# The first attention head and its value block are loaded ahead of the attention section, and the planner prices a transfer by its bytes

## The chip, the cores and the metric

The kernel runs on one core of a Trainium2 chip. The metric is device time in microseconds (us) of one launch, the median of several runs. The engines named below are TensorE (PE: matrix products and transposes), VectorE (DVE), ScalarE (ACT), GpSimd (POOL) and SyncE (SP), which here only issues transfers (DMAs) between the chip's memory and the on-chip buffers. Each engine works through its own instructions strictly in program order, and so does SP's list of transfers.

## What is computed

One layer of a decoder, on 16 learned tokens and 1024 tokens of width 1024. Cut to what the change touches:

```python
h = rms_norm(concat(meta_tokens, x), g_pre_mix) @ w_in          # 8 blocks of 1024 features
b_c, c_c, h_c, q, k, v, g_conv, g_attn = split(h)
branch_conv = (b_c * causal_dwconv(c_c * h_c)) @ w_proj_conv
# stick-breaking attention, 16 heads of 64 features, query blocks of 128
z    = q_block @ k.T / 8
beta = log_sigmoid(z)
fail = where(s < t, beta - z, 0)
a    = where(s < t, exp(beta + reverse_cumsum(fail) - fail), 0)
branch_attn = concat(a @ v) @ w_proj_attn
merged = sigmoid(g_conv + b0) * branch_conv + sigmoid(g_attn + b1) * branch_attn
h = h + rms_norm(merged @ w_out, g_post_mix)
# then a gated MLP with a depthwise convolution, and its own norms
```

Every product is done in float32 accuracy from split operands: a matrix is rounded to a high part, the rest is kept as a low part, and three matmuls (high by high, high by low, low by high) make one product.

## The kernel before

**Stages.** A short prologue normalises and turns the tokens into features (`xnT`). The *projection section* then makes the feature blocks of `w_in`, 128 features at a time: some blocks plainly, 21 pairs of blocks by a Strassen-like scheme with seven products on halves, for which four sums of token halves are kept split in the tiles T1 to T4 (`tpool`). Queries, keys and values go to the chip's memory (`qh_d`, `ql_d`, `kh_d`, `kl_d`, `vv_d`), and later come back one head at a time. The last block of this section is the *bridge*: one gate block (`bridge_gate`), done plainly, 72 matmuls from `xnT` alone. The *attention section* works through 8 pairs of heads, and 12 more gate blocks (`mid_gates`) are threaded between as filler for TensorE. The output projections and the MLP follow.

**Attention, per head.** A head's queries and keys (`qh`, `ql`, `kk`) are six transfers of 64 rows; a pair's values (`vv`) are two transfers. For nine query blocks in three groups: scores `z` (PE, two matmuls for a chunk), `fl` = sigmoid(-z) (ACT, L970), a scan along the keys (DVE, L981), transposes `tp` (PE, L1000), a high part `ah` (ACT, L1005) and a low part `al` (DVE, L447), and the weighted values `av` (PE, L1015 and L1016).

**A gate block** needs its weights: a transfer `raw` (L358), a cast `whi` on ACT (L457), a low part `wlo` on POOL (L369), then 72 matmuls (L345 to L347) in three chunks, each ended by a sigmoid on ACT (L670) into `gt`; the whole is stored by SP (L673).

**What sets the order.** Both sections are written through a planner (`Plan`): tasks with an engine, a cost, a key, dependences and slots (buffers). It plays them through with those costs; whenever an engine is free it takes the ready task with the lowest key, and the instructions are emitted in that order and then held to it. The costs thus decide only which instruction stands before which. Before the change each SP task cost 0.4, a head 2.4 and a value block 0.8, with a lag of 3.5 until its data counts as there. The projection section and the attention section are two separate plans, and each starts with an idle SP.

**Buffers around the change.** The pool `heads` (three buffers each of `qh`, `ql`, `kk`, two of `vv`) is opened where the tiles T1 to T4 lay, after the first plan was emitted. The pool `work`, with the `fl` tiles, is opened where the projection section's ring of output tiles (`su`, `hi`, `gt`) lay; a tile of `work` may be written only when the stores that read the old tile there have ended.

The plan's first gate after the bridge (`nxt`, i = 0 of the mid gates) has its weights loaded and split in the projection section already. Below it is *gate 0*; *gate 1* is the first whose `raw` is loaded in the attention section.

Of the kernel before, what the change touches and what calls it, by code (L numbers as in the profile page):

```python
# [11 lines left out]
F32 = mybir.dt.float32  # L12
# [5 lines left out]
P = 128  # L18
D = 1024
# [14 lines left out]


class Plan:
    LAG = {"PE": 0.22, "ACT": 0.18, "DVE": 0.13, "POOL": 0.13, "SP": 3.5, None: 0.0}

    def __init__(self, slots):
        self.slots = dict(slots, port=1)  # L40
# [89 lines left out]

def any_cost(n):
    return {"DVE": dve_cost(n), "POOL": pool_cost(n)}


@with_exitstack
def block_kernel(ctx, tc, x, meta_tokens, g_pre_mix, w_in, channels, w_proj_conv,
# [312 lines left out]
    def plain(o, chunks, key, make, evac, finish, psum, first_chunk=0, given=None, eng="ANY"):  # L449
        st = {}  # L450
        if given is None:
            def load():
                st["raw"] = load_raw(o)

            def high():
                st["hi"], st["lo"] = whole(st["raw"])
                nc.scalar.copy(st["hi"], st["raw"])  # L457

            ld = plan.add("SP", 0.4, load, key=key - 16, takes=("raw",))
            h = plan.add("ACT", act_cost(D), high, (ld,), key - 10, ("whi", "wlo"))  # L460
            los = [plan.add(eng, any_cost(512) if eng == "ANY" else pool_cost(512),
                            lambda e="POOL", i=i: lo_piece(st["raw"], st["hi"], st["lo"], i, e, 512), (h,),
                            key - 9 + 3 * i) for i in range(2)]
            plan.join(los, ("raw",))
        else:
            st["hi"], st["lo"], los = given
        before, evacs = None, []
        for ci in range(first_chunk, 3):
            a, n = chunks[ci]
# [58 lines left out]
    def done_b(cb, u, after, key):  # L528
        y, after2 = mixed.pop(("y", cb))

        def product(e):
            engine_of(e).tensor_tensor(y()[:, :NQ], y()[:, :NQ], u()[:, T0:], op=ALU.mult)

        t = plan.add("ANY", any_cost(NQ), product, tuple(after) + tuple(after2), key + 4)
        plan.join((t,), ("wk",))
        plan.add("SP", 0.4, lambda: nc.sync.dma_start(y_d[cb * P:(cb + 1) * P, :], y()[:, :NQ]),
                 (t,), key + 5, (), ("wk",))

    def done_qk(hi_d, lo_d, t0):
        def done(p, u, after, key):  # L540
# [6 lines left out]
            def lower(e):  # L547
# [4 lines left out]
            s1 = plan.add("SP", 0.4, lambda: nc.sync.dma_start(hi_d[rows, :], st["hi"].bitcast(F32)), (h,), key + 4)  # L552
            plan.join((s1, t), ("wk",))
            plan.add("SP", 0.4, lambda: nc.sync.dma_start(lo_d[rows, :], u()[:, t0:]),
                     (t,), key + 5, (), ("wk",))
        return done

    def done_v(p, u, after, key):
# [15 lines left out]
        for k0, kn, m in ((0, 4, P), (4, 4, P), (8, 1, QB)):  # L574
# [28 lines left out]
            plan.add("SP", 0.4, store, (w,), key + 7, (), ("wk",))  # L603
        plan.join(turned, ("wk",))

    def token_op(name, kb, a, n):
# [56 lines left out]
    def gate_out(which, ob, tile_of, space):  # L663
        u = {}

        def make():
            u["t"] = tile_of()

        def evac(a, n, ps):
            nc.scalar.activation(u["t"][:, a - T0:a - T0 + n], ps, AF.Sigmoid, bias=bias_gate(which, ob))  # L670

        def finish(after, key):
            plan.add("SP", 0.4, lambda: nc.sync.dma_start(  # L673
                (gc_d, ga_d)[which][ob * P:(ob + 1) * P, :], u["t"][:, :NQ]), tuple(after), key, (), space)
        return make, evac, finish

# [54 lines left out]
    def strassen_pair(i, at):  # L731
# [14 lines left out]
        ld = [plan.add("SP", 0.4, lambda j=j: load(j), (), at - 30, ("raw",)) for j in range(2)]  # L746

        def keep(name, src, after):
            def high():
# [82 lines left out]
        for k in range(7):  # L832
            pair = []
            for s in range(2):
# [18 lines left out]
                else:  # L853
                    p[6, s] = product(6, s, "b1", False, "T4", (p["e", s],))
                    evac(s, 1, 0, "b1", None, (p[6, s],), p[6, s].key, ("st",))
            plan.join((p[k, 0], p[k, 1]), (tags[names[k]],))
        for o in range(2):
            _, k, done = pairs1[i][o]
            done(k, late_tile(u[o]), evacs[o], at + (12 + o) * prod)

    snap_free = {}
    for i in range(len(pairs1)):
        strassen_pair(i, at)
        at += 14 * prod
# [14 lines left out]
    ld = plan.add("SP", 0.4, next_load, (), at - 20, ("raw",))  # L879
# [14 lines left out]
    heads_ctx = ctx.enter_context(ExitStack())  # L894
    heads = heads_ctx.enter_context(pool("heads", 3))
    work_ctx = ctx.enter_context(ExitStack())
    work = work_ctx.enter_context(pool("work", 2, "right"))
    upper = work.tile([QB, NT], F32, name="upper", tag="upper", bufs=1)
# [2 lines left out]
                            compare_op=ALU.is_gt, fill=1.0, base=0, channel_multiplier=1)  # L901

    FL = [2] * 6 + [1] * 3
    plan = Plan({"raw": 2, "whi": 1, "wlo": 1, "mm": 2, "z": 2, "tp": 3, "av": 1, "qk": 3, "vv": 2,
                 "ot": 2, "wk": 2, "ah": 4, "al": 4, "half": 1, **{f"fl{b}": n for b, n in enumerate(FL)}})
    plan_bank = "mm"
    units = [(p, h, g) for p in range(NPAIR) for h in range(2) for g in range(3)]
# [5 lines left out]
        starts[u] = t  # L913
        t += share[u[2]] * half_pair
    DELAY = 0.6 * half_pair
    vload, out_tiles = {}, {}
    av_last = last_turn = None
    for p in range(NPAIR):
        ot_parts = []
        vst = {}  # L920

        def load_v(p=p, vst=vst):
            vst["vv"] = heads.tile([P, 9, 2, P], F32R, name="vv", tag="vv", bufs=2)
            nc.sync.dma_start(vst["vv"][:, 0:8].bitcast(F32), vv_d[p, :, 0:8])
            nc.sync.dma_start(vst["vv"][:QB, 8:9].bitcast(F32), vv_d[p, :QB, 8:9])

        v_ld = None
        v_users = []
        for h in range(2):
            hst = {}  # L930

            def load_h(p=p, h=h, hst=hst):
                r = slice(p * P + 64 * h, p * P + 64 * h + 64)
                qh, ql = (heads.tile([P, NQ], F32R, name=n, tag=n) for n in ("qh", "ql"))
                kk = heads.tile([P, NT], F32R, name="kk", tag="kk")
                for z0 in (0, 64):
                    zs = slice(z0, z0 + 64)
                    nc.sync.dma_start(qh[zs].bitcast(F32), qh_d[r, :])
                    nc.sync.dma_start(kk[zs].bitcast(F32), (kl_d if z0 else kh_d)[r, :])
                    nc.sync.dma_start(ql[zs].bitcast(F32), ql_d[r, :])  # L940
                hst["q"] = (qh, ql, kk)

            t_h = starts[p, h, 0]
            h_ld = plan.add("SP", 2.4, load_h, (), t_h - 40, ("qk",))
            if h == 0:
                v_ld = plan.add("SP", 0.8, load_v, (), t_h - 35, ("vv",))
            z_users = []
            for g in range(3):
                t_u = starts[p, h, g]
                scans, fls = {}, {}  # L950
                for b in range(3 * g, 3 * g + 3):
# [6 lines left out]
                    while c0 < nk:  # L958
                        n = min(wch, nk - c0)

                        def scores(c0=c0, n=n, q0=q0, bst=bst, hst=hst):
                            qh, ql, kk = hst["q"]
                            z = bst["z", c0] = ps_z.tile([P, 512], F32, name="z", tag="z")[:QB, :n]
                            nc.tensor.matmul(z, qh[:, q0:q0 + QB], kk[:, c0:c0 + n], start=True, stop=False)
                            nc.tensor.matmul(z, ql[:, q0:q0 + QB], kk[:, c0:c0 + n], start=False, stop=True)
# [23 lines left out]
                for kb in range(nkb):  # L989
# [21 lines left out]
                    def weigh(kb=kb, n=n, off=off, h=h, nkb=nkb, kst=kst, ust=ust, vst=vst):  # L1011
                        if kb == 0:
                            ust["av"] = ps_av.tile([P, 512], F32, name="av", tag="av")[:, :CH]
                        av, w = ust["av"], vst["vv"][:n, kb, h, :]
                        nc.tensor.matmul(av[:, off:], w, kst["ah"][:n, off:], start=(kb == 0), stop=False)  # L1015
                        nc.tensor.matmul(av[:, off:], w, kst["al"][:n, off:], start=False,  # L1016
                                         stop=(kb == nkb - 1))
# [38 lines left out]
        def last_add(e="POOL", p=p):  # L1056
# [4 lines left out]
        plan.add("SP", 0.4, lambda p=p: nc.sync.dma_start(o_d[p * P:(p + 1) * P, :], out_tiles[p][:, :NQ]),  # L1061
                 (fin,), t_o + 1, (), ("ot",))

    for i, (which, ob) in enumerate(mid_gates):
# [721 lines left out]
```

## Time and profile before

| | |
|---|---|
| time, median of 3 runs | 2003.27 us (2003.04 to 2005.58) |
| the profiled execution's own time | 2005.19 us |
| its span, first to last instruction | 2003.3 us |
| mean granted TensorE clock | 0.987 |
| projection section ends (bridge's last matmul) | 551.0 us into the span |
| last product of the attention section | about 970 us |

The profile is one execution. Busy PE includes the pipeline depth of each matmul, so in a dense stretch records overlap and the spacing of their starts (0.16 us for a matmul of 342 columns) is the pace. The view of waits lists idle time of an engine by what ended it. The view by stretches gives busy time per engine, the granted clock (1.00 is full speed) and how busy the 16 DMA engines were. The timeline gives instructions by start; SPq is SP's issue of a transfer, not the transfer.

### The profile page before, as it was taken

The numbers are of one execution on the slowest core, as the hardware profiler recorded it, in microseconds if no ns is written. First come the engines' busy times: TensorE is split into PE (matmuls) and PEld (weight loads), VectorE is DVE, ScalarE is ACT, GpSimd is POOL, SyncE is SP. The second block draws the span as 40 slices with busy tenths as digits, with TensorE's granted clock in tenths as the row PEclk, the third lists the DMA queues.
The fourth block names the chain that finished last, engine by engine and source line by source line (L and its number), as shares of the span: only waits on it lengthen the run. The fifth ranks groups of instructions, "written<-read, shape, count | busy, mean of one in ns | idle before, by whom it ended". The sixth has DMA issues, their size and how long they took to land.

```text
span 2003.3 us, 32045 instructions
## 1 busy us (share of the span) xinstructions
PE 1922.9 (96%) x12732; PEld 1809.7 (90%) x12732; DVE 1129.5 (56%) x1730; ACT 838.2 (42%) x1766; POOL 646.9 (32%) x486
## 2 busy tenths in 40 slices
PE   6999999999959999999899999989999999999997
PEld 6999999999959999999799999879988998888886
DVE  6846666655428878787541126874444444355547
ACT  5533343444326667666531223453443344321122
POOL 1110000001112323223223550354656465654353
PEclk9999999999979999999999999999999999999999
DMA  3522221455575554541484673213222222253224
GB/s 139 163 85 75 75 75 50 143 153 158 145 197 142 127 148 130 140 130 43 147 241 155 197 196 113 89 44 112 77 72 81 88 79 70 95 177 107 84 85 136
DMA packets 73842, 238.55 MB, mean 119 GB/s; under 512 B 15401, under 2 KB 17225, under 8 KB 72669
## 3 DMA queue, kind: packets, MB, share of 16 engines
q1 hardware_dynamic: 70368, 226.00, 37.6%
q10 hardware_dynamic: 3324, 10.50, 1.7%
q8 instruction: 100, 1.64, 0.4%
q14 instruction: 50, 0.40, 0.1%
HBM read 166.02 MB, written 70.46 MB: 118 GB/s over the span
## 4 chain that ended last, share of the span: by engine, by line
PE 76%; DVE 10%; DMA 6%; ACT 3%; POOL 3%; issue 2%; SPq 0%; ACTq 0%; DVEq 0%; POOLq 0%
PE st L798 7%; PE st L795 7%; PE st L797 7%; PE st L1402 6%; PE st L1406 5%; PE st L1404 5%; DVE fl L981 3%; PE st L1696 3%; PE st L1694 3%; PE st L1695 3%; PE tp L1000 2%; PE mm L245 2%; PE mm L246 2%; PE mm L247 2%; PE mm L345 2%
## 5 line engine op out<-in xcount | busy, mean ns | idle before, releaser
L981 DVE TENSOR_TENSOR_SCAN fl<-fl,upper 114x470 f32<-114x470 f32 (+3 forms) x144 | 207.8, 1461 | 37.3 <-ACT fl L970 36.7
L173 POOL TENSOR_TENSOR a_op<-raw,a_op 128x512 fp32r<-128x512 f32 (+1 forms) x136 | 192.8, 1431 | 87.8 <-ACT a_op L172 85.6
L795 PE MATMUL st<-tT,s_op 128*128 128x260 f32 x672 | 190.9, 284 | 0.0
L798 PE MATMUL st<-tT,s_op 128*128 128x260 f32 x672 | 190.1, 283 | 0.0
L797 PE MATMUL st<-tT,s_op 128*128 128x260 f32 x672 | 190.0, 283 | 0.0
L1402 PE MATMUL st<-opT,a_op 128*128 128x258 f32 (+2 forms) x528 | 171.0, 324 | 5.6 <-ACT snap L1417 3.1
L1404 PE MATMUL st<-opT,a_op 128*128 128x258 f32 (+2 forms) x528 | 169.0, 320 | 2.6 <-DVE opT L173 1.7
L1406 PE MATMUL st<-opT,a_op 128*128 128x258 f32 (+2 forms) x528 | 168.8, 320 | 0.0
L447 DVE TENSOR_TENSOR al<-tp,ah 114x342 fp32r<-114x342 f32 (+3 forms) x288 | 116.4, 441 | 78.5 <-ACT ah L1005 77.6
L172 ACT CAST a_op<-raw 128x512 fp32r<-128x512 f32 (+1 forms) x136 | 85.1, 634 | 156.0 <-DMA raw<-in_w_up_gate_dram 52.7
L1701 DVE TENSOR_TENSOR acc<-acc,st 128x512 f32<-128x512 f32 x144 | 98.5, 687 | 91.1 <-PE st L1696 91.1
L795 PE MATMUL st<-xnT,s_op 128*128 128x260 f32 x504 | 142.4, 283 | 0.0
L798 PE MATMUL st<-xnT,s_op 128*128 128x260 f32 x504 | 142.3, 282 | 0.0
L797 PE MATMUL st<-xnT,s_op 128*128 128x260 f32 x504 | 141.8, 281 | 0.0
L1005 ACT CAST ah<-tp 114x342 fp32r<-114x342 f32 (+3 forms) x288 | 106.0, 405 | 83.1 <-PE tp L1000 75.8
L176 DVE TENSOR_TENSOR raw<-raw 128x512 f32<-128x512 f32 x72 | 72.7, 1010 | 108.0 <-POOL a_op L173 106.3
L751 ACT CAST s_op<-raw 128x512 fp32r<-128x512 f32 x126 | 77.9, 622 | 130.8 <-PE st L798 117.5
L1045 POOL TENSOR_TENSOR ot<-ot,half 64x342 f32<-64x342 f32 x48 | 59.8, 1246 | 211.1 <-ACT ot L1041 211.0
L1402 PE MATMUL st<-opB,a_op 128*128 128x512 f32 (+2 forms) x396 | 127.4, 322 | 0.0
L1404 PE MATMUL st<-opB,a_op 128*128 128x512 f32 (+2 forms) x396 | 127.4, 322 | 0.0
L1406 PE MATMUL st<-opB,a_op 128*128 128x512 f32 (+2 forms) x396 | 126.9, 321 | 0.0
L798 PEld LDWEIGHTS st<-tT,s_op 128*128 128x128 f32 x672 | 126.8, 189 | 0.0
(222 smaller groups left out, 5898.5 us busy)
## 6 DMA issues: line engine op xcount, KB each, us to landing
raw<-in_w_in_dram SPq DMA_DIRECT2D x64, 512.0 KB
raw<-in_w_up_gate_dram SPq DMA_DIRECT2D x44, 512.0 KB
act_d<-owork SPq DMA_DIRECT2D x22, 512.0 KB
araw<-act_d SPq DMA_DIRECT2D x22, 512.0 KB
raw<-in_w_down_dram SPq DMA_DIRECT2D x22, 512.0 KB
qh<-qh_d SPq DMA_DIRECT2D x32, 256.5 KB
ql<-ql_d SPq DMA_DIRECT2D x32, 256.5 KB
vv_d<-vt SPq DMA_DIRECT2D x16, 512.0 KB
```

The costliest lines, as they stand in the source:

```text
L172: nc.scalar.copy(hi, src)
L173: (lo_engine or nc.vector).tensor_tensor(lo, src, hi.bitcast(F32), op=ALU.subtract)
L447: eng.tensor_tensor(out, src, hi.bitcast(F32), op=ALU.subtract)
L795: nc.tensor.matmul(ps, wt[:, 0, c], xh, start=start and kb == 0, stop=False, skip_group_check=True)
L797: nc.tensor.matmul(ps, wt[:, 0, c], xl, start=False, stop=False, skip_group_check=True)
L798: nc.tensor.matmul(ps, wt[:, 1, c], xh, start=False, stop=kb == 3, skip_group_check=True)
L981: nc.vector.tensor_tensor_scan(fl[:, ::-1], fl[:, ::-1], upper[:, NT - nk:][:, ::-1], 1.0, op0=ALU.mult, op1=ALU.max)
L1005: nc.scalar.copy(kst["ah"][:n, off:], kst["tp"][:n, off:CH])
L1402: nc.tensor.matmul(ps, wt[:, 0, k], xh, start=start and kb == 0, stop=False, skip_group_check=True)
L1404: nc.tensor.matmul(ps, wt[:, 0, k], xl, start=False, stop=False, skip_group_check=True)
L1406: nc.tensor.matmul(ps, wt[:, 1, k], xh, start=False, stop=stop and kb == 3, skip_group_check=True)
L1701: nc.vector.tensor_tensor(a, a, ps, op=ALU.add)
```

## The change

It has four parts. (1) Head (0,0) and the value block of pair 0 are loaded by two tasks of the first plan, which depend on the products of the last Strassen pair; at that point the T tiles are closed and the pool `heads` is opened. The second plan therefore holds two slots for heads and one for values at its start, and frees the others when head 0 and pair 0 are done. (2) All SP tasks cost their bytes (`dma_cost`): 7.6 for a head, 5.6 for a value block, 2.5 for a block of weights or a store; the lag is 2.5. (3) In a head's six transfers the two of `ql` go last. (4) Some names change (`load_head`, `load_values` instead of closures). No arithmetic changes.

```diff
-    LAG = {"PE": 0.22, "ACT": 0.18, "DVE": 0.13, "POOL": 0.13, "SP": 3.5, None: 0.0}
+    LAG = {"PE": 0.22, "ACT": 0.18, "DVE": 0.13, "POOL": 0.13, "SP": 2.5, None: 0.0}
...
+def dma_cost(n):
+    return max(0.3, 512 * n / 210000.0)
...
-            ld = plan.add("SP", 0.4, load, key=key - 16, takes=("raw",))
+            ld = plan.add("SP", dma_cost(D), load, key=key - 16, takes=("raw",))
...
+        if i == len(pairs1) - 1:
+            last_products.extend(p[k, s] for k in range(7) for s in range(2))
...
+    def open_heads():
+        t_ctx.close()
+        heads["pool"] = heads_ctx.enter_context(pool("heads", 3))
+
+    def load_head(p, h):
+        r = slice(p * P + 64 * h, p * P + 64 * h + 64)
+        qh, ql = (heads["pool"].tile([P, NQ], F32R, name=n, tag=n) for n in ("qh", "ql"))
+        kk = heads["pool"].tile([P, NT], F32R, name="kk", tag="kk")
+        for z0 in (0, 64):
+            zs = slice(z0, z0 + 64)
+            nc.sync.dma_start(qh[zs].bitcast(F32), qh_d[r, :])
+            nc.sync.dma_start(kk[zs].bitcast(F32), (kl_d if z0 else kh_d)[r, :])
+        for z0 in (0, 64):
+            nc.sync.dma_start(ql[z0:z0 + 64].bitcast(F32), ql_d[r, :])
+        head_tiles[p, h] = qh, ql, kk
...
+    opened = plan.add(None, 0.0, open_heads, last_products)
+    t = plan.add("SP", dma_cost(3 * NT), lambda: load_head(0, 0), (opened,), at)
+    plan.add("SP", dma_cost(9 * 256), lambda: load_values(0), (opened, t), at + 1)
     which, ob = bridge_gate
     plain(48 + 8 * which + ob, CH_Q, at, *gate_out(which, ob, lambda: wk_tile("gt"), ("wk",)), bank)
...
-    plan = Plan({"raw": 2, "whi": 1, "wlo": 1, "mm": 2, "z": 2, "tp": 3, "av": 1, "qk": 3, "vv": 2,
+    plan = Plan({"raw": 2, "whi": 1, "wlo": 1, "mm": 2, "z": 2, "tp": 3, "av": 1, "qk": 2, "vv": 1,
...
-            h_ld = plan.add("SP", 2.4, load_h, (), t_h - 40, ("qk",))
-            if h == 0:
-                v_ld = plan.add("SP", 0.8, load_v, (), t_h - 35, ("vv",))
+            h_ld = None
+            if (p, h) != (0, 0):
+                h_ld = plan.add("SP", dma_cost(3 * NT), lambda p=p, h=h: load_head(p, h), (), t_h - 40,
+                                ("qk",))
+            if h == 0 and p > 0:
+                v_ld = plan.add("SP", dma_cost(9 * 256), lambda p=p: load_values(p), (), t_h - 35,
+                                ("vv",))
```

What this does to the order is seen at three places.

**The end of the projection section, SP.** Before: the last four stores of queries and keys, the bridge's gate store (`ga_d`), then head 0.

```order
L552 DMA qh_d<-hi 128x1026
L554 DMA ql_d<-su 128x1026
L552 DMA kh_d<-hi 128x1040
L554 DMA kl_d<-su 128x1040
L673 DMA ga_d<-gt 128x1026
L938 DMA qh<-qh_d 64x1026
L939 DMA kk<-kh_d 64x1040
L940 DMA ql<-ql_d 64x1026
```

Now:

```order
L556 DMA qh_d<-hi 128x1026
L885 DMA qh<-qh_d 64x1026
L886 DMA kk<-kh_d 64x1040
L885 DMA qh<-qh_d 64x1026
L886 DMA kk<-kl_d 64x1040
L888 DMA ql<-ql_d 64x1026 x2
L893 DMA vv<-vv_d 128x2048
L894 DMA vv<-vv_d 114x256
L558 DMA ql_d<-su 128x1026
L556 DMA kh_d<-hi 128x1040
L558 DMA kl_d<-su 128x1040
L677 DMA ga_d<-gt 128x1026
```

Head 0 and the value block stand ahead of three stores and of the bridge's store. Behind these rows both lists go on with heads 1 and 2 and the value block of pair 1 (now with gate 0's store ahead of that block), and then the first weights:

```order
L925 DMA vv<-vv_d 114x256
L358 DMA raw<-in_w_in_dram 128x1024 x2
L673 DMA ga_d<-gt 128x1026
L358 DMA raw<-in_w_in_dram 128x1024
L938 DMA qh<-qh_d 64x1026
```

is now

```order
L894 DMA vv<-vv_d 114x256
L362 DMA raw<-in_w_in_dram 128x1024
L885 DMA qh<-qh_d 64x1026
L886 DMA kk<-kh_d 64x1040
L885 DMA qh<-qh_d 64x1026
L886 DMA kk<-kl_d 64x1040
L888 DMA ql<-ql_d 64x1026 x2
L362 DMA raw<-in_w_in_dram 128x1024 x3
```

The first `raw` (gate 1's) still follows heads 1, 2 and the value block; the second no longer stands beside it but behind head 3.

**The start of the attention section, PE.** Here `st` is the bridge and `mm` gate 0. Before, 39 matmuls of gate 0 stood between the bridge's last row and the first score; the last of them and the first scores read

```order
L347 MATMUL mm<-xnT,wlo 128x342
L964 MATMUL z<-kk,qh 114x128
L965 MATMUL z<-kk,ql 114x128
L964 MATMUL z<-kk,qh 114x242
L965 MATMUL z<-kk,ql 114x242
L345 MATMUL mm<-xnT,whi 128x342
```

Now the first score follows the bridge at once, and gate 0 is spread between the scores of head 0:

```order
L351 MATMUL st<-xnT,wlo 128x342
L978 MATMUL z<-kk,qh 114x128
L979 MATMUL z<-kk,ql 114x128
L349 MATMUL mm<-xnT,whi 128x342
L350 MATMUL mm<-xnT,whi 128x342
```

From the first score on, 72 matmuls of gate 0, 58 of scores, 39 transposes and 28 of weighted values stand ahead of gate 1's first matmul; before, that matmul came already among head 0's scores. From the 392nd PE instruction behind the bridge's last row on, PE's list reads the same in both kernels to the end, and the 391 ahead of it are in both 171 of gates, 76 of scores, 84 transposes and 60 of weighted values, in another order. The 398th, which opens a run of six products `av`, serves below as the meeting point.

**The cast of gate 1's weights, ACT.** Before (with `gt` gate 0's third sigmoid):

```order
L970 ACTIVATE fl<-z 114x350
L970 ACTIVATE fl<-z 114x348
L457 CAST whi<-raw 128x1024
L670 ACTIVATE gt<-mm,par 128x342
L457 CAST whi<-raw 128x1024
L970 ACTIVATE fl<-z 114x406 x2
L1005 CAST ah<-tp 128x342
```

There the casts of gates 1 and 2 stood in front of the seventh query block's `fl` of head 0 and of the first `ah`. Now the cast of gate 1 stands behind all of head 0, six query blocks of head 1 and two of head 2:

```order
L984 ACTIVATE fl<-z 114x128
L984 ACTIVATE fl<-z 114x242
L461 CAST whi<-raw 128x1024
L1019 CAST ah<-tp 114x342 x3
L984 ACTIVATE fl<-z 114x356
L984 ACTIVATE fl<-z 114x470
```

In the projection section PE's list is the same row for row. On ACT, DVE and POOL some casts and subtractions change places, most of them among the first pieces of T1 to T4, and some subtractions change engine.

More of the change, by code (lines that the diff above doesn't have):

```diff
@@ L535, in done_b @@
         plan.join((t,), ("wk",))
-        plan.add("SP", 0.4, lambda: nc.sync.dma_start(y_d[cb * P:(cb + 1) * P, :], y()[:, :NQ]),
+        plan.add("SP", dma_cost(NQ), lambda: nc.sync.dma_start(y_d[cb * P:(cb + 1) * P, :], y()[:, :NQ]),
                  (t,), key + 5, (), ("wk",))
@@ L551, in done @@
             t = plan.add("ANY", any_cost(n), lower, (h,), key + 4)
-            s1 = plan.add("SP", 0.4, lambda: nc.sync.dma_start(hi_d[rows, :], st["hi"].bitcast(F32)), (h,), key + 4)
+            s1 = plan.add("SP", dma_cost(n), lambda: nc.sync.dma_start(hi_d[rows, :], st["hi"].bitcast(F32)), (h,), key + 4)
             plan.join((s1, t), ("wk",))
-            plan.add("SP", 0.4, lambda: nc.sync.dma_start(lo_d[rows, :], u()[:, t0:]),
+            plan.add("SP", dma_cost(n), lambda: nc.sync.dma_start(lo_d[rows, :], u()[:, t0:]),
                      (t,), key + 5, (), ("wk",))
@@ L602, in done_v @@
             w = plan.add("DVE", dve_cost(kn * P), lower, (h,), key + 6, (), ("st",))
-            plan.add("SP", 0.4, store, (w,), key + 7, (), ("wk",))
+            plan.add("SP", dma_cost(kn * 256), store, (w,), key + 7, (), ("wk",))
         plan.join(turned, ("wk",))
@@ L672, in finish @@
         def finish(after, key):
-            plan.add("SP", 0.4, lambda: nc.sync.dma_start(
+            plan.add("SP", dma_cost(NQ), lambda: nc.sync.dma_start(
                 (gc_d, ga_d)[which][ob * P:(ob + 1) * P, :], u["t"][:, :NQ]), tuple(after), key, (), space)
@@ L744, in a @@
             return r[j][:, 512 * s:512 * s + 512]
-        ld = [plan.add("SP", 0.4, lambda j=j: load(j), (), at - 30, ("raw",)) for j in range(2)]
+        ld = [plan.add("SP", dma_cost(D), lambda j=j: load(j), (), at - 30, ("raw",)) for j in range(2)]
         def keep(name, src, after):
@@ L859, in strassen_pair @@
             done(k, late_tile(u[o]), evacs[o], at + (12 + o) * prod)
-    snap_free = {}
+    snap_free, last_products = {}, []
     for i in range(len(pairs1)):
@@ L864, in block_kernel, with load_values @@
         at += 14 * prod
+    head_tiles, v_tiles, heads = {}, {}, {}
+    heads_ctx = ctx.enter_context(ExitStack())
+    def open_heads():
[12 more added lines that the diff above has]
+        head_tiles[p, h] = qh, ql, kk
+    def load_values(p):
+        vv = v_tiles[p] = heads["pool"].tile([P, 9, 2, P], F32R, name="vv", tag="vv", bufs=2)
+        nc.sync.dma_start(vv[:, 0:8].bitcast(F32), vv_d[p, :, 0:8])
+        nc.sync.dma_start(vv[:QB, 8:9].bitcast(F32), vv_d[p, :QB, 8:9])
+    opened = plan.add(None, 0.0, open_heads, last_products)
+    t = plan.add("SP", dma_cost(3 * NT), lambda: load_head(0, 0), (opened,), at)
+    plan.add("SP", dma_cost(9 * 256), lambda: load_values(0), (opened, t), at + 1)
     which, ob = bridge_gate
@@ L877, in next_high @@
         nc.scalar.copy(nxt["hi"], nxt["raw"])
-    ld = plan.add("SP", 0.4, next_load, (), at - 20, ("raw",))
+    ld = plan.add("SP", dma_cost(D), next_load, (), at - 20, ("raw",))
     h = plan.add("ACT", act_cost(D), next_high, (ld,), at - 10, ("whi", "wlo"))
@@ L893, in block_kernel @@
     ps_av = psA.enter_context(pool("ps_av", 1, space=PSUM))
-    heads_ctx = ctx.enter_context(ExitStack())
-    heads = heads_ctx.enter_context(pool("heads", 3))
     work_ctx = ctx.enter_context(ExitStack())
@@ L915, in block_kernel @@
     DELAY = 0.6 * half_pair
-    vload, out_tiles = {}, {}
+    out_tiles = {}
     av_last = last_turn = None
@@ L919, in block_kernel @@
         ot_parts = []
[L920 to L925, printed above, removed]
         v_ld = None
@@ L929, in block_kernel @@
         for h in range(2):
[L930 to L941, printed above, removed]
-            t_h = starts[p, h, 0]
-            h_ld = plan.add("SP", 2.4, load_h, (), t_h - 40, ("qk",))
-            if h == 0:
-                v_ld = plan.add("SP", 0.8, load_v, (), t_h - 35, ("vv",))
+            t_h = starts[p, h, 0]
+            h_ld = None
[5 more added lines that the diff above has]
+                                ("vv",))
             z_users = []
@@ L959, in block_kernel, with scores @@
                         n = min(wch, nk - c0)
-                        def scores(c0=c0, n=n, q0=q0, bst=bst, hst=hst):
-                            qh, ql, kk = hst["q"]
+                        def scores(c0=c0, n=n, q0=q0, bst=bst, p=p, h=h):
+                            qh, ql, kk = head_tiles[p, h]
                             z = bst["z", c0] = ps_z.tile([P, 512], F32, name="z", tag="z")[:QB, :n]
@@ L1009, in lower, with weigh @@
                         low(nc.vector, kst["al"][:n, off:], kst["tp"][:n, off:CH], kst["ah"][:n, off:])
-                    def weigh(kb=kb, n=n, off=off, h=h, nkb=nkb, kst=kst, ust=ust, vst=vst):
+                    def weigh(kb=kb, n=n, off=off, h=h, nkb=nkb, kst=kst, ust=ust, p=p):
                         if kb == 0:
                             ust["av"] = ps_av.tile([P, 512], F32, name="av", tag="av")[:, :CH]
-                        av, w = ust["av"], vst["vv"][:n, kb, h, :]
+                        av, w = ust["av"], v_tiles[p][:n, kb, h, :]
                         nc.tensor.matmul(av[:, off:], w, kst["ah"][:n, off:], start=(kb == 0), stop=False)
@@ L1060, in block_kernel @@
         fin = plan.add("POOL", pool_cost(NQ), last_add, tuple(ot_parts), t_o + 1)
-        plan.add("SP", 0.4, lambda p=p: nc.sync.dma_start(o_d[p * P:(p + 1) * P, :], out_tiles[p][:, :NQ]),
+        plan.add("SP", dma_cost(NQ), lambda p=p: nc.sync.dma_start(o_d[p * P:(p + 1) * P, :], out_tiles[p][:, :NQ]),
                  (fin,), t_o + 1, (), ("ot",))
```

1 line of the change is left out of this document (removed).

## The prediction

> **What bounds the kernel now.** First the page's busy times and its chain of work that ended last:
>
> ```profile
> PE 1922.9 (96%) x12732; PEld 1809.7 (90%) x12732; DVE 1129.5 (56%) x1730; ACT 838.2 (42%) x1766; POOL 646.9 (32%) x486
> ...
> PE 76%; DVE 10%; DMA 6%; ACT 3%; POOL 3%; issue 2%; SPq 0%; ACTq 0%; DVEq 0%; POOLq 0%
> ```
>
> TensorE is the bound of nearly every stretch, so only what makes it wait, or slows its clock, costs time. The change works on one place where it waits, the passage into attention. Second, PE's waits between 551 and 640 us:
>
> ```profile
> PE z L964 <- ACT fl L970: 15.6, 1, 15.6
> PE z L964 <- DMA kk<-kl_d: 5.1, 1, 5.1
> PE z L965 <- DMA ql<-ql_d: 0.9, 1, 0.9
> PE av L1016 <- DVE al L447: 0.4, 1, 0.4
> ```
>
> A score waits 5.1 us for head 0's keys and its partner 0.9 us for the low queries; later a score waits 15.6 us for a sigmoid on ACT. The timeline tells why:
>
> ```profile
> 538.56 0.33 SPq L552 DMA_DIRECT2D qh_d<-hi  x1
> 551.78 0.32 SPq L673 DMA_DIRECT2D ga_d<-gt  x1
> 552.19 0.51 SPq L938 DMA_DIRECT2D qh<-qh_d  x1
> 576.48 1.63 SPq L358 DMA_DIRECT2D raw<-in_w_in_dram  x2
> ...
> 588.01 1.04 ACT L457 CAST whi<-raw 128x1024 fp32r<-128x1024 f32 x1 [14.96 <-DMA raw<-in_w_in_dram]
> ...
> 550.86 0.32 PE L347 MATMUL st<-xnT,wlo 128*128 128x342 f32 x1
> 551.01 0.32 PE L345 MATMUL mm<-xnT,whi 128*128 128x342 f32 x1
> 562.42 0.42 PE L964 MATMUL z<-kk,qh 128*114 128x128 f32 x1 [5.14 <-DMA kk<-kl_d]
> 590.90 0.73 PE L964 MATMUL z<-kk,qh 128*114 128x464 f32 x1 [15.64 <-ACT fl L970]
> 636.46 0.32 PE L1015 MATMUL av<-ah,vv 114*128 114x342 f32 x1
> ```
>
> SP may issue head 0 only after the bridge's store (551.78). The sigmoid stands on ACT behind the cast of gate 1's weights, and that cast waits 14.96 us because `raw` lands at 588.0, behind heads 0 to 2 and two value blocks. So one queue of transfers is the true bound of this passage. Third, the stretches:
>
> ```profile
> core 0: us, PE busy (x) PEld busy (x) DVE busy (x) ACT busy (x) POOL busy (x), PEclk, DMA share, GB/s
> 538.00:551.00 13.00, 13.00 (x88) 13.00 (x87) 2.47 (x2) 3.38 (x6) 1.25 (x2) 1.00 0.78 164
> 551.00:564.00 13.00, 6.92 (x43) 6.51 (x42) 0.00 (x0) 1.10 (x2) 0.00 (x0) 0.94 0.87 228
> 564.00:576.00 12.00, 11.26 (x58) 10.84 (x58) 6.11 (x6) 3.76 (x9) 0.00 (x0) 0.78 1.04 224
> 576.00:591.00 15.00, 0.10 (x1) 0.10 (x1) 0.00 (x0) 2.99 (x5) 1.86 (x2) 0.62 0.80 220
> 591.00:600.00 9.00, 9.00 (x45) 8.72 (x46) 6.70 (x9) 5.32 (x15) 4.06 (x4) 0.69 0.29 87
> ```
>
> The DMA engines are full from 551 to 588 at 220 to 228 GB/s, and after each long wait the clock is down while PE works: 12 us at 0.78 lose 2.6 us, 9 us at 0.69 lose 2.8 us, together **5.4 us**.
>
> **The path before.** From the bridge's end (551.01) to the meeting point, the 398th PE instruction behind it (636.46), pass 85.4 us. Without the three long waits (21.6) and the clock's loss (5.4) there remain 58.4 us of work for 397 instructions, 0.147 us each. What can be gained here is at most those 27.0 us.
>
> **Head 0 moved ahead of the bridge.** It removes the 5.1 and 0.9 us if it lands by 551.0. The sizes:
>
> ```profile
> qh<-qh_d SPq DMA_DIRECT2D x32, 256.5 KB
> vv_d<-vt SPq DMA_DIRECT2D x16, 512.0 KB
> vv<-vv_d SPq DMA_DIRECT2D x8, 1024.0 KB
> kl_d<-su SPq DMA_DIRECT2D x8, 520.0 KB
> kk<-kh_d SPq DMA_DIRECT2D x16, 260.0 KB
> ga_d<-gt SPq DMA_DIRECT2D x8, 513.0 KB
> vv<-vv_d SPq DMA_DIRECT2D x8, 114.0 KB
> raw<-in_w_in_dram SPq DMA_DIRECT2D x64, 512.0 KB
> ```
>
> A head is 4 x 256.5 + 2 x 260 = 1546 KB, a value block 1138 KB. Before, 7939 KB (gate store, three heads, two value blocks, one `raw`) pass from 551.78 to 588.01, 219 KB/us; with half of the second `raw`, which travels beside the first, 226. Now the queue starts at 538.56 with the `qh_d` store and head 0: 2059 KB at 219 land at 548.0, or at 551.4 at the 164 GB/s (160 KB/us) of the first stretch. I take 549: the first score follows the bridge at once.
>
> **Gate 1's weights.** No transfer is saved; they only start earlier. Ahead of `raw` and with it now go the `qh_d` store (513), head 0 (1546), a value block (1138), three stores (1553), the bridge's store (513), heads 1 and 2 (3092), gate 0's store (513), a value block (1138) and `raw` (512): 10518 KB. At 219 to 226 KB/us it lands at 586.6 to 585.1. The planner does not see this backlog, since the second plan starts with an idle SP. I take **586.0**, 2 us before the old 588.0.
>
> **What PE does until then.** Ahead of gate 1's first matmul stand 197 instructions, at 0.147 us 29.0 us: it could start at 580.0. Before, it came among head 0's scores; so the wait is not gone but met with more work done. After the cast ACT has three casts `ah` and two sigmoids ahead of the scores that PE needs first:
>
> ```profile
> L1005 ACT CAST ah<-tp 114x342 fp32r<-114x342 f32 (+3 forms) x254 | 93.6, 406 | 75.5 <-PE tp L1000 68.3 <-DVE fl L981 6.4
> L970 ACT ACTIVATE fl<-z 114x348 f32<-114x348 f32 (+8 forms) x210 | 91.7, 477 | 12.7 <-PE z L965 12.6
> L369 POOL TENSOR_TENSOR wlo<-raw,whi 128x512 fp32r<-128x512 f32 x22 | 32.9, 1514 | 99.1 <-ACT whi L457 63.5 <-PE z L965 35.6
> ```
>
> 586.0 + 1.04 + 3 x 0.41 + 2 x 0.48 = 589.2; eight PE instructions (1.2) bring gate 1 to **590.5**. The low half on POOL (1.5 us from 587.0) is hidden beside them. PE idles some 10.5 us between 551 and 590.5, in pieces: bounds 0 (rate high) and 24 (164 GB/s). I take one clock loss of 2.7 us, half of the old two, between 0 and 5.4.
>
> **DVE and the buffers as cover.** The scores of head 0 now wait for `work` buffers that the `kh`, `kl` and gate stores still read; with the bridge's store 5263 KB are through, at 562 to 563, and the fifth block's sigmoid, due near 560, waits for it. From there DVE has five scans of head 0, six short ones of head 1 and 14 low parts:
>
> ```profile
> L981 DVE TENSOR_TENSOR_SCAN fl<-fl,upper 114x356 f32<-114x356 f32 (+3 forms) x128 | 185.1, 1466 | 10.5 <-ACT fl L970 10.1
> L447 DVE TENSOR_TENSOR al<-tp,ah 114x342 fp32r<-114x342 f32 (+3 forms) x254 | 102.4, 440 | 54.7 <-ACT ah L1005 53.9
> ```
>
> Scaled by their columns (5256 a head for 9 x 1.466 us) that is 10.2 + 6.2 + 14 x 0.44 = 22.6 us, until about 586. This is hidden behind `raw` and its cast, by some 4 us, and is the next wait if `raw` comes early.
>
> **Other edits, at nothing.** The low queries last in a head: heads after the second are loaded ahead. The changed order in the projection section: PE's list there is the same, and operand making runs ahead of PE, held by it:
>
> ```profile
> ACT s_op L751 <- PE st L798: 121.9, 57, 2.3
> ```
>
> If that cover failed among the first pieces, a few us either way. After the meeting point the lists are the same on PE.
>
> **Sum.** 590.5 + 200 x 0.147 + 2.7 = 622.6, against 636.46: **13.9 us** gained. The span 2003.3 becomes 1989.4 and the profiled execution (2005.19, 1.9 more) 1991.3. The shown median, 2003.27, lies 1.9 below that execution; less 13.9 it gives **1989.4**.
>
> A rule for the clock: the Trainium skill, "TensorE: Matmul & The Clock Gate", section "HAM oscillation — how this bites in real kernels", warns of PE gaps over about 3.4 us; by it, waits cut into shorter pieces cost no clock, and the sum would be 2.7 us lower. The trace agrees for gaps of 5.1 and 15.6 us; it has no run of shorter ones.
>
> **Rivals.**
> - *The wait is gone.* If the transfers run faster, gate 1 starts at 580.0 with the clock up: 609.4 at the meeting point, 27 us gained, **1976**. For it: the queue starts 13 us earlier. Against it: the engines are full at 220 to 228 GB/s in three stretches, and DVE needs its 22.6 us. The Trainium skill, "DMA: Bandwidth & Descriptors", section "Measured (HBM→SBUF, 128 partitions, SWDGE, issued from GpSimd)", gives 341 GB/s at 1 MB, by which, as an estimate, `raw` would land near 570; these rows stay at two thirds of that.
> - *Head 0 does not come earlier*: if its buffers, where the T tiles lay, came free only with the bridge, all behind the `qh_d` store starts at 551.8 as before: 10005 KB until 596.9, gate 1 10.9 us later, 3 us gained, **2000**. Against it: the bridge reads `xnT`, not the T tiles.
> - *Slower: the queue is slow with stores in it.* `raw` now stands behind six stores. At the 164 GB/s of 538 to 551 (four stores, nothing else) it lands at 604.3, gate 1 comes 18 us later than forecast, and the time is **2008**. It decides below 172 KB/us (176 GB/s). Against it: that stretch was full only 0.78 of the time, so the stores ran at some 210 GB/s when busy.
>
> **How the numbers follow.** Forecast (8 to 19 us gained) 0.66; wait gone 0.12; head 0 not earlier, or other new waits that leave 0 to 7 us, 0.16; slower 0.06. The range leaves out most of the wait-gone and slower cases: 1981 to 1999. Less than 0.2%, 4.0 us, is about what a measurement here can't tell from no change: faster 0.87 (forecast, wait gone, part of the third), same 0.08, slower 0.05.
>
> **What would show it.** The waits for `kk` and `ql` gone; the `whi` cast still idle on `raw` until about 586; gate 1's first matmul near 590; the 398th instruction near 622.6; the DMA engines full from 539 to 586. Wrong if PE waits in the projection section, if the first score starts after 552, or if `raw` lands before 581 or after 592.

## The result, and the profile after

The changed kernel takes **1992.55 us** in the median of 4 runs (1991.95 to 1994.74), the kernel before 2003.71 us beside it: 11.2 us less, a ratio of 0.9945 with a 95% interval of 0.9928 to 0.9962. A second measurement (e9 below) gave 1990.66 against 2002.88 us, 12.2 us less, ratio 0.9938 (0.9926 to 0.9951). The forecast was 1989.4 us, 13.9 us less. The profiled execution has a span of 1993.0 us and a time of 1994.74 us. First the page's busy times and chain of work, which hardly differ from before:

```profile
PE 1923.2 (96%) x12732; PEld 1807.2 (91%) x12732; DVE 1135.0 (57%) x1732; ACT 838.8 (42%) x1766; POOL 648.8 (33%) x484
...
PE 76%; DVE 10%; DMA 7%; ACT 3%; POOL 2%; issue 2%; ACTq 0%; DVEq 0%; SPq 0%; POOLq 0%
```

The same work is done on every engine; what changed is the passage into attention. PE's waits there, from 551 to 640 us (in total, times, longest):

```profile
PE z L978 <- ACT fl L984: 9.4, 4, 7.0
PE av L1029 <- ACT ot L1055: 0.4, 1, 0.4
```

The waits for `kk` (5.1 us) and `ql` (0.9) are gone, the one for a sigmoid fell from 15.6 us in one piece to 9.4 in four. The timeline of the changed kernel (start, duration, engine, line, operation, idle time before it and what ended that):

```profile
539.50 1.02 SPq L885 DMA_DIRECT2D qh<-qh_d  x1
552.31 0.32 SPq L677 DMA_DIRECT2D ga_d<-gt  x1
573.29 0.34 SPq L362 DMA_DIRECT2D raw<-in_w_in_dram  x1
574.51 0.45 SPq L885 DMA_DIRECT2D qh<-qh_d  x1
580.76 5.21 SPq L888 DMA_DIRECT2D ql<-ql_d  x2
...
564.91 0.72 ACT L984 ACTIVATE fl<-z 114x292 f32<-114x292 f32 x2 [5.38 <-DMA ga_d<-gt]
590.23 1.04 ACT L461 CAST whi<-raw 128x1024 fp32r<-128x1024 f32 x1 [6.64 <-DMA raw<-in_w_in_dram]
...
551.38 0.32 PE L351 MATMUL st<-xnT,wlo 128*128 128x342 f32 x1
551.53 0.22 PE L978 MATMUL z<-kk,qh 128*114 128x128 f32 x1
565.38 0.42 PE L978 MATMUL z<-kk,qh 128*114 128x350 f32 x1 [1.76 <-ACT fl L984]
592.74 0.59 PE L978 MATMUL z<-kk,qh 128*114 128x292 f32 x1 [7.02 <-ACT fl L984]
594.99 0.49 PE L349 MATMUL mm<-xnT,whi 128*128 128x342 f32 x1
625.65 0.32 PE L1029 MATMUL av<-ah,vv 114*128 114x342 f32 x1
```

Read it from SP down. Head 0 is issued at 539.50, and the first score follows the bridge's last matmul at once (551.53). Gate 1's weights are issued at 573.29 and land at 590.23, where their cast starts; the six loads of head 3 are issued right behind them, from 574.51 on. The cast again stands ahead of the sigmoids that PE waits for, so PE waits 7.02 us. Gate 1 starts at 594.99, and the meeting point comes at 625.65 instead of 636.46, 10.8 us earlier; the spans differ by 10.3. The stretches show the clock (the third last column), and last the stretch in which gate 1's weights are in flight:

```profile
551.00:564.00 13.00, 12.52 (x80) 12.00 (x78) 3.12 (x4) 2.68 (x6) 0.00 (x0) 1.00 1.03 277
564.00:576.00 12.00, 10.04 (x54) 8.70 (x55) 8.39 (x10) 8.00 (x21) 0.00 (x0) 0.86 1.03 239
576.00:591.00 15.00, 9.01 (x63) 7.54 (x60) 10.41 (x15) 7.52 (x20) 2.54 (x2) 0.98 1.03 219
591.00:600.00 9.00, 7.26 (x35) 7.25 (x36) 6.13 (x8) 3.29 (x9) 2.51 (x2) 0.65 0.64 146
...
592.74:600.00 7.26, 7.26 (x35) 7.24 (x36) 5.04 (x6) 1.55 (x4) 1.12 (x1) 0.69 0.59 145
...
573.30:590.20 16.90, 11.37 (x81) 9.69 (x79) 13.11 (x18) 8.68 (x24) 2.54 (x2) 1.00 1.03 227
```

PE now works 9.01 of the 15 us from 576 to 591, where before it worked 0.10. But the clock is down twice. 12 us at 0.86 lose 1.7. Behind the 7.02 us wait, 7.26 us at 0.69 lose 2.2 (the 9 us at 0.65 would be 3.2, but PE still stood idle for 1.7 of them).

### The profile page after: what moved, and what is told of

Its sections match the earlier page's. It is cut to its first block, busy times and chain, and to the rows that moved or that the text cites. A ratio compares the mean times of both kernels' runs of the same rounds, so it can differ in the third digit from the quotient of the medians.

```text
span 1993.0 us, 32046 instructions
## 1 busy us (share of the span) xinstructions
PE 1923.2 (96%) x12732; PEld 1807.2 (91%) x12732; DVE 1135.0 (57%) x1732; ACT 838.8 (42%) x1766; POOL 648.8 (33%) x484
## 4 chain that ended last, share of the span: by engine, by line
PE 76%; DVE 10%; DMA 7%; ACT 3%; POOL 2%; issue 2%; ACTq 0%; DVEq 0%; SPq 0%; POOLq 0%
PE st L799 7%; PE st L802 7%; PE st L801 7%; PE st L1416 7%; PE st L1420 6%; PE st L1418 6%; PE st L1710 3%; PE st L1708 3%; PE st L1709 3%; DVE fl L995 3%; PE mm L249 2%; PE mm L251 2%; PE mm L250 2%; PE tp L1014 2%; DMA xv<-in_x_dram 2%; PE mm L349 2%
## 5 line engine op out<-in xcount | busy, mean ns | idle before, releaser
L995 DVE TENSOR_TENSOR_SCAN fl<-fl,upper 114x470 f32<-114x470 f32 (+4 forms) x144 | 208.7, 1468 | 33.1 <-ACT fl L984 32.7
```

Source lines behind the costliest of these rows:

```text
L995: nc.vector.tensor_tensor_scan(fl[:, ::-1], fl[:, ::-1], upper[:, NT - nk:][:, ::-1], 1.0, op0=ALU.mult, op1=ALU.max)
```

## The experiments

Two questions stand. Which edit brings the gain, the early load or the planner's prices? And why do gate 1's weights land 4 us later than forecast? All times are medians, each ratio is to the kernel before, measured on the same chip:

| run | edit | us | before, us | ratio (95%) |
|---|---|---|---|---|
| e1 | early head alone | 1997.34 | 2003.35 | 0.9976 (0.9965 to 0.9987) |
| e2 | new prices alone | 1987.26 | 2003.35 | 0.9918 (0.9905 to 0.9932) |
| e3 | changed kernel, head 3 later | 1983.51 | 2003.35 | 0.9903 (0.9890 to 0.9917) |
| e4 | changed kernel, gate 1's weights first | 1985.31 | 2003.35 | 0.9907 (0.9894 to 0.9921) |
| e5 | changed kernel, value block behind the stores | 1990.93 | 2003.43 | 0.9939 (0.9926 to 0.9952) |
| e6 | changed kernel, backlog in the planner | 1981.25 | 2003.43 | 0.9890 (0.9876 to 0.9903) |
| e7 | e6 and e3 | 1980.62 | 2003.43 | 0.9885 (0.9871 to 0.9900) |
| e8 | e6 and e4 | 1980.72 | 2003.43 | 0.9889 (0.9876 to 0.9903) |
| e9 | changed kernel | 1990.66 | 2002.88 | 0.9938 (0.9926 to 0.9951) |
| e10 | e6 and e5 | 1977.86 | 2002.88 | 0.9879 (0.9866 to 0.9893) |
| e11 | e6, e4 and e5 | 1978.17 | 2002.88 | 0.9875 (0.9860 to 0.9890) |

### The two halves of the change apart (e1, e2)

In e1 the changed kernel gets the old prices back:

```diff
-    LAG = {..., "SP": 2.5, None: 0.0}
+    LAG = {..., "SP": 3.5, None: 0.0}
 def dma_cost(n):
-    return max(0.3, 512 * n / 210000.0)
+    return {3 * NT: 2.4, 9 * 256: 0.8}.get(n, 0.4)
```

> The changed kernel with the planner's old prices for transfers (0.4, 2.4 and 0.8 us, lag 3.5): only the early load of head 0 is left. In its list gate 1's first matmul stands 98 PE instructions behind the bridge (197 with the new prices). Theory (the gain of the change comes from what PE does while it waits for gate 1's weights, and so from gate 1's later place, which the new prices made): the waits for kk and ql are gone, but PE reaches gate 1's place near 566 and waits until its weights have landed; 10005 KB go ahead of them from 538.6 on, at 219 to 226 KB/us 583 to 585, resumed near 589, and 300 PE instructions and 2.7 us of slow clock are left to the meeting point near 636: the time is 2000 to 2004 us, at most 3 us under before. Rival (the early head is what pays; the new prices do nothing here): 1991 to 1994 us, as the whole change.

In e2 the kernel before gets `LAG["SP"]` 2.5 and `dma_cost` at every transfer, and keeps its loads of heads and values where they were.

> The kernel before with the new prices and the new lag, and nothing else: head 0 is loaded behind the bridge's store as before. Its first score stands 67 PE instructions behind the bridge (40 before), gate 1's first matmul 265 (100 before). Theory (the later place of gate 1 pays): the score for head 0 comes near 561 and hardly waits for its keys, the weights of gate 1 land at 589 to 594 (8452 KB ahead and with them from 551.8 on) and PE has work until then, held back by the scans that start late; a wait of 0 to 8 us is left, and the time is 1984 to 1996 us. Rival (without the early head the new prices do nothing): 2000 to 2006 us.

Measured: 1997.34 us for the early head alone, between the two expectations, and 1987.26 us for the prices alone, within the theory's and **3 to 5 us under the whole change** (1990.66 and 1992.55). The intervals of the ratios touch, so the profiles have to carry this as well: from the start of the bridge's last row to the 398th PE instruction behind it pass 68.0 us in e2, 74.3 in the changed kernel and 71.6 in e9 (85.6 before). e1's timeline and its longest waits, then e2's waits:

```profile
583.48 1.04 ACT L461 CAST whi<-raw 128x1024 fp32r<-128x1024 f32 x1 [17.38 <-DMA raw<-in_w_in_dram]
584.94 0.68 PE L978 MATMUL z<-kk,qh 128*114 128x406 f32 x1 [15.00 <-ACT fl L984]
```

```profile
PE z L978 <- ACT fl L984: 15.0, 1, 15.0
PE z L979 <- DMA ql<-ql_d: 1.9, 1, 1.9
```

```profile
PE av L1020 <- DVE al L451: 2.1, 3, 1.1
PE z L968 <- DMA kk<-kl_d: 1.2, 1, 1.2
PE z L969 <- DMA ql<-ql_d: 1.0, 1, 1.0
PE z L968 <- ACT fl L974: 0.7, 3, 0.3
```

With the early head alone gate 1 stands 98 instructions behind the bridge, and PE waits 15.00 us at a score behind its cast, nearly the old 15.64, only 6.0 us earlier (584.94 against 590.90); the time fell by 6.0. That is not the waits for `kk` and `ql` (6.0 us before): `ql` is still awaited for 1.9 us in e1. The weights land 4.5 us earlier (583.48 against 588.01), and the sigmoid follows their cast 1.4 us sooner. The expected 2000 to 2004 had the landing right, but reckoned with the changed kernel's ACT list behind the cast; here the awaited sigmoid follows it within 1.5 us. With the prices alone no wait for the cast is left at all: gate 1 stands 265 instructions behind the bridge, and PE has work until its weights are there.

So the two halves work against each other. Alone they gain 6.0 and 16.1 us, together 11 to 12. In the changed kernel the second plan starts with head 0 already loaded and an idle SP, and puts gate 1 at 197 instead of 265.

### The planner told of the backlog (e6)

```diff
     DELAY = 0.6 * half_pair
+    plan.add("SP", 10.0, None, key=-1000.0)
```

> The changed kernel with 10 us of work that isn't there put at the head of SP's list in the second plan: the planner then sees about the backlog that the queue has. Loads stay in their order; gate 1's first matmul moves from 197 to 253 PE instructions behind the bridge, its cast from ACT's 45th to 66th place. Theory (head of line: the early head costs nothing by itself; it only made the planner put gate 1 too early for its weights): PE reaches gate 1 near 592, when the weights are there, the 7.0 us wait and the slow clock behind it (3.2 us) are gone, and the time is 1980 to 1985 us, under both the changed kernel and the new prices alone (1987.3). Rival (the early head itself costs, by its loads ahead of the stores): 1986 to 1990 us, no better than the new prices alone.

Measured: 1981.25 us, in the theory's range. Its waits in the passage, and the cast, which now waits for nothing:

```profile
PE av L1031 <- DVE al L451: 2.0, 3, 0.9
PE z L979 <- ACT fl L985: 0.7, 2, 0.5
```

```profile
591.09 1.06 ACT L461 CAST whi<-raw 128x1024 fp32r<-128x1024 f32 x1
```

Up to gate 2's weights the loads stand in the same order as in the changed kernel, and the cast starts later than there (591.09 against 590.23); some 9 to 11 us are gained because other work stands ahead of it. The gain over the kernel before, 22.2 us, is as large as that of the two halves alone together (6.0 and 16.1), though e1's 6.0 came about in another way. The rival's range is missed: e6 is 6 us under the new prices alone. e2's waits for `kk` and `ql` (2.2 us) and the slow clock behind them (12 us at 0.86, 1.7 us) are gone in e6: this is what the early head brings, 3.9 of the 6 us. The new prices with the 10 us but without the early head were not run, so what the 10 us would do there is not shown.

### What delays gate 1's weights (e3)

```diff
...
+                if last_head is not None:
+                    last_head.users.append(h_ld)
+                    h_ld.left += 1
+                head_loads[p, h] = last_head = h_ld
...
+    gate_loads[-9].users.append(head_loads[1, 1])
+    head_loads[1, 1].left += 1
     plan.run()
```

`gate_loads` lists the loads of gate weights in their order, and `gate_loads[-9]` is that of gate 3's; heads keep their order among themselves.

> The changed kernel with head 3's six loads behind the weights of gate 3 instead of right behind those of gate 1; PE's list differs by 8 rows. Only gate 2's weights (512 KB) can travel beside gate 1's. Theory A (head 3, issued 1.2 us behind gate 1's weights, shares the DMA engines with them and delays them by some 4 us): the weights land at 585 to 587.5, the wait ahead of them is 3 to 5 us shorter, and the time 2 to 5 us under the changed kernel, near 1989. Theory B (what stands ahead is slow by itself, and what is issued behind doesn't matter): they land at 589.5 to 591 again, and the time is within 1.5 us of the changed kernel.

Measured: 1983.51 us, 7 to 9 us under the changed kernel. Theory A's direction, with twice its size. The timeline of e3 (its first row takes three issues together, at 571.93, 573.83 and 587.16), then its stretch from 576 to 591 us and the one in which the weights are in flight:

```profile
571.93 15.56 SPq L362 DMA_DIRECT2D raw<-in_w_in_dram  x3
583.49 1.04 ACT L463 CAST whi<-raw 128x1024 fp32r<-128x1024 f32 x1 [2.77 <-DMA raw<-in_w_in_dram]
586.00 0.39 PE L985 MATMUL z<-kk,qh 128*114 128x292 f32 x1 [3.12 <-ACT fl L991]
587.58 0.45 SPq L888 DMA_DIRECT2D qh<-qh_d  x1
```

```profile
576.00:591.00 15.00, 11.41 (x67) 10.41 (x67) 13.65 (x19) 8.40 (x20) 6.90 (x6) 0.89 0.61 205
...
571.90:583.50 11.60, 9.93 (x68) 8.40 (x67) 11.54 (x18) 7.58 (x23) 2.55 (x2) 1.00 0.91 286
```

From issue to cast the weights take 11.56 us here and 16.94 in the changed kernel, behind the same transfers. Elsewhere, too, it goes with what is issued behind: 11.5 us before and 11.11 in e1 (only other weights behind them), 15.31 in e9 and 17.23 in e5 (head 3 behind); 13.15 in e4, where heads 1 and 2 stand behind them and a shorter queue ahead.

The view by stretches, taken from the start of the queue to the cast, tells what was moved: 11.31 MB in e3 (44.52 us at 254 GB/s), 11.97 in the changed kernel (51.15 us at 234) and 12.01 in e9 (48.83 us at 246). What stands ahead of the weights and they themselves are 10518 KB (of 1024 bytes), or 10.77 MB. So 0.5 MB of later transfers were moved in e3, which is gate 2's weights, and 1.2 MB in the other two. The 0.7 MB more take 2.6 to 2.8 us at e3's rate. The rest is the rate, which differs by 12 GB/s between two executions of the changed kernel, too; what sets it these runs do not settle.

The remaining wait is 3.1 us instead of 7.0, and the clock behind it loses 1.7 us (15 at 0.89) instead of 2.2.

Once gate 1 stands later, this no longer matters:

> The kernel with the planner's 10 us, and head 3 behind the weights of gate 3 as well. Theory (both edits remove the same wait): the weights land near 584, nothing waits for them, and the time is within 1.5 us of the one with the 10 us alone. Rival (they add up): 1972 to 1976 us.

Measured: 1980.62 us, 0.6 under e6: the two edits remove the same wait.

### Gate 1's weights first (e4, e8)

```diff
...
+            if i == 1:
+                gate_loads[-1].key = -100
     plan.run()
```

> The changed kernel with the weights of gate 1 loaded first behind the bridge's store, ahead of heads 1 and 2 and the value block; the planner then puts gate 1 102 PE instructions behind the bridge. Theory (the landing of these weights is what holds the passage): they land at 564 to 568, their cast waits no more, PE waits less than 5 us in all up to the meeting point, which comes near 613, and the time is 1978 to 1984 us. Rival (the queue as a whole or DVE binds as well: what was put behind, head 1 first, is then awaited, or DVE's scans are): the waits come back at head 1's first score or at the transposes, and the time is 1988 to 1994 us.

Measured: 1985.31 us, between the two ranges. The cast, and the wait behind it:

```profile
565.80 1.04 ACT L463 CAST whi<-raw 128x1024 fp32r<-128x1024 f32 x1 [9.01 <-DMA raw<-in_w_in_dram]
567.36 0.59 PE L981 MATMUL z<-kk,qh 128*114 128x292 f32 x1 [7.17 <-ACT fl L987]
```

The weights land at 565.8, as the theory had it, but the wait doesn't go: the planner moved the cast to ACT's fifth place, ahead of sigmoids that could have run. The rival's waits, for head 1 or the scans, did not come either. In e8 the planner's 10 us move the cast to the 19th place:

> The kernel with gate 1's weights first behind the bridge's store, and the planner's 10 us: its cast moves from ACT's 5th to 19th place, gate 1 from 102 to 128 PE instructions. Theory (the 7.2 us wait of that kernel was the cast standing ahead of sigmoids until 565.8): the cast comes at 566 to 569 with under 2 us of waiting, PE's wait is gone, and the time is 1976 to 1982 us. Rival (the fourth and fifth blocks' sigmoids wait for their buffers and the stores anyway, and head 1 lands later): 1983 to 1986 us, as without the 10 us.

Measured: 1980.72 us, as the theory said. The cast comes at 569.44 and waits for nothing. The longest wait left for a sigmoid is 1.5 us, the one for the bridge's store.

### The buffers that the stores hold (e5, e10, e11)

```diff
-    plan.add("SP", dma_cost(9 * 256), lambda: load_values(0), (opened, t), at + 1)
...
     plan.run()
+    load_values(0)
     psS.close()
```

> The changed kernel with head 0's value block loaded behind the bridge's store, not ahead of the last three operand stores; all lists of PE, ACT and DVE are the same, and the bytes ahead of gate 1's weights too. The bridge's store lands 5.2 us earlier (1138 KB at 219 KB/us), so ACT's wait for it (5.4 us), PE's wait behind that (1.8 us) and the slow clock from 566 to 570 (1.7 us) should go. Theory (the weights of gate 1 end last, so what is gained ahead of them is waited for in front of them): they land at 588 to 591, PE's longest wait grows from 7.0 to about 10 us, and the time is within 1.5 us of the changed kernel's 1992.6. Rival (each wait costs its own length): 1988 to 1990 us.

Measured: 1990.93 us, against 1992.55 and 1990.66 of the changed kernel: 1.6 us under the first, just outside the theory's 1.5, and 0.3 above the second; the changed kernel's own two measurements differ by more. The waits of e5 decide for the theory:

```profile
PE z L978 <- ACT fl L984: 10.9, 4, 10.1
PE av L1029 <- ACT ot L1055: 0.4, 1, 0.4
```

The 1.76 us wait is gone and the last one has grown from 7.0 to 10.1, since the weights land at 588.97. What is gained ahead of the last transfer is waited for in front of it. Where that wait is gone, the same edit pays:

> The changed kernel itself, unedited, on the same chip as the two that follow, to carry their comparison and to see whether its gain repeats. Theory (the gain is 10.8 us, half of the clear road from 2003.5 to about 1980): 1991 to 1994 us, gate 1's cast idle on its weights for 6 to 7 us, and the clock down behind that wait. Rival (the first measurement was an outlier, and the prediction's 1989.4 is the true time): 1988 to 1990.5 us.

> The kernel with the planner's 10 us, and head 0's value block behind the bridge's store. Theory (a wait removed ahead of the weights pays once the weights are no longer awaited): ACT's 5.1 us wait for the store and PE's 0.5 us behind it go, the scans start some 5 us earlier, but the weights land near 588 to 590 and gate 1 stands at the same place; 0 to 2 us under 1981.3, so 1979 to 1981.5 us. Rival (PE now comes to gate 1 before its weights): 1982 to 1986 us, with a wait of 3 us or more for a sigmoid behind the cast.

> The kernel with the planner's 10 us and gate 1's weights first, and head 0's value block behind the bridge's store: PE's four waits of 2.7 us for sigmoids shrink, as the buffers that the stores hold come free 5 us earlier. Theory (nothing in the passage is awaited then): 2 to 3 us under 1980.7, so 1977.5 to 1979 us, the lowest of all. Rival (the passage is at the floor that TensorE's own work sets, or DVE's scans hold it): 1980 to 1981.5 us, no change.

Measured: 1990.66 us for the changed kernel again, just under the theory's range and just above the rival's, so its gain repeats, and the forecast lies 1.3 us beside it; 1977.86 us in e10, below both ranges (3.4 under e6, or 2.8 when each is compared with the kernel before measured beside it); 1978.17 us in e11, in the theory's range. The waits of e10, which with e11 is the best of all versions:

```profile
PE av L1031 <- DVE al L451: 2.0, 3, 0.9
PE z L979 <- ACT fl L985: 0.3, 1, 0.3
```

Against e9 on the same chip e10 gains 12.8 us, by one line for the planner and one load put behind the stores.

## Why the prediction was right, and which sizes were off

- **What bounds the passage** (one queue of transfers, with gate 1's weights last): right. e5 shows it by a gain that vanishes, e3 by a wait that shrinks when the weights land earlier, e6 by one that goes when more work stands ahead of their cast.
- **Head 0 early**: right. The first score follows the bridge at once, and both waits for `kk` and `ql` (6.0 us) are gone. That e1 gains 6.0 as well is chance: `ql` is awaited there.
- **Gate 1's weights at 586.0**: too early by 4.2 us in the profiled execution (590.2) and by 2.6 in e9 (588.57). The sum counted the 10518 KB ahead of them and with them, and nothing behind. By the cast 1.2 MB of later loads, head 3's above all, had been moved as well: 5 us at the measured 234 GB/s, and e3 shows that without head 3 behind them the weights land earlier. This is the term that was mis-sized. It is more than the whole difference between 13.9 and 11.2; a part came back behind gate 1.
- **Gate 1 at 590.5**: it came at 594.99. From the cast to the first awaited score it took 2.5 us, not 3.2; the eight instructions then took 2.25, not 1.2, at half the clock.
- **One clock loss of 2.7 us**: two were there. The one behind the 7.02 us wait cost 2.2 us. The other, 1.7 us, followed the 1.76 us wait, which the prediction did not reckon with as a gap; it lies ahead of the wait for the weights, and e5, which is without it, is no faster. In e9 that wait is 0.71 us and no loss follows, so this part differs between executions of the same kernel. The prediction also read its trace as holding no shorter gaps. Outside the passage it holds one: a wait of 2.04 us that ends at 1172.81 is followed by a clock of 0.76 over 7.2 us.
- **After gate 1**: 200 instructions and the clock were forecast at 32.1 us, and took 30.7 (594.99 to 625.65).
- **The buffers held by the stores**: right in place and nearly in time (562 to 563 forecast, the sigmoid at 564.9). Its cover is the wait for the weights, and e10 shows what it costs when that cover is gone, some 3 us. DVE was the next wait, as forecast, but a small one: 1.7 to 2.0 us for `al` in e6, e8 and e10.
- **Other edits at nothing**: nothing in the runs speaks against it, but no run takes the place of `ql` in a head's loads by itself. The span behind the meeting point is 1367.3 us, before 1366.8, and 1365.2 in e9, so it differs by 2 us between executions of the same kernel.
- **The meeting point**: 625.65 for 622.6. Gate 1 4.5 us late, less 1.4 gained behind it.
- **Rivals**: the wait did not go (1976), since the cast stays ahead of the sigmoids and the weights land late; in e6, e7, e8, e10 and e11, where it does go, the times are 1977.9 to 1981.3. Head 0 was earlier (not 2000), the queue was not slow (not 2008).

What the prediction had seen, that the planner doesn't know of the backlog, is the larger part of the story, and it drew no number from it: it took the 197 instructions as given and did not ask where the prices alone would have put gate 1. That is 16.1 us alone, and with the early head beside them 11 to 12 are left.

## What to carry to other kernels

When a planner sets the order, ask of each edit what the planner will believe afterwards: a load that is moved out of its sight makes it put the consumers of the next loads too early, and an instruction that waits for a transfer holds all that stand behind it on its engine. It was cheaper here to tell the planner of the backlog (10 us that aren't there) than to speed up the transfer. Count what is issued behind a transfer too, and when a wait in front of it is removed, expect nothing until the transfer itself is no longer the last.

## What the runs showed of the hardware

**Gaps and the clock.** PE's wait near 565 us differs between the runs. After 0.47, 0.71, 1.47 and 1.54 us (e6, e9, e8, e7) the granted clock stayed at 1.00 in 564 to 576 us; after 1.76 us (the changed kernel) it was 0.86, as in e2 after 1.24 and 0.96 us within 1.3 us of each other. In e1, where PE waits 1.85 us for `ql`, it was 0.87 in 551 to 564 us. The window and the wait of e7:

```profile
564.00:576.00 12.00, 9.66 (x62) 8.19 (x63) 9.99 (x10) 9.05 (x25) 1.00 (x1) 1.00 1.04 241
```

```profile
565.18 0.41 PE L986 MATMUL z<-kk,qh 128*114 128x350 f32 x1 [1.54 <-ACT fl L992]
```

The length of a wait alone does not decide it. Near the end of the attention section one product `av` waits 1.42 to 1.45 us for `al` in all 13 traces. Behind it the clock stayed up in eleven of them and went down in two, e2 and e8. The kernel before, then e8:

```profile
960.55 0.43 PE L1016 MATMUL av<-al,vv 128*128 128x342 f32 x1 [1.44 <-DVE al L447]
960.50:972.50 12.00, 11.92 (x83) 10.98 (x84) 5.84 (x14) 6.60 (x17) 2.54 (x4) 1.00 0.13 39
```

```profile
937.84 0.53 PE L1034 MATMUL av<-al,vv 128*128 128x342 f32 x1 [1.43 <-DVE al L451]
937.80:949.80 12.00, 11.89 (x73) 10.93 (x74) 5.82 (x14) 6.13 (x16) 1.16 (x3) 0.86 0.02 3
```

The Trainium skill, "TensorE: Matmul & The Clock Gate", section "HAM oscillation — how this bites in real kernels", warns of gaps over about 3.4 us. Here gaps of half of that and less were followed by a lower clock in some traces, so the measurement decides; what besides the length decides it is open.

**Transfers issued later.** Weights of 512 KB took 11.1 to 11.6 us from issue to use with other weights behind them (the kernel before, e1, e3), and 15.3 to 17.2 us with a head's six loads behind them (the changed kernel, e9, e5). The Trainium skill, "DMA: Bandwidth & Descriptors", section "Queues, rings and completion order", states that each DMA engine takes the descriptors of a ring in order, but with no barrier between them, so that a later one may finish its write before an earlier one. These runs agree in so far as 1.2 MB of later loads were moved before the weights were used, where head 3 stood behind them, and 0.5 MB where it did not; the order within one DMA engine no run here shows.
